# A gated decoder layer on one core: T2 in own tiles at the second turn, later stores of forced jobs, spread loads, the last multiply of the recurrence on VectorE

## The chip, the core and the metric

The kernel runs on one core of a Trainium2 chip. The metric is the device time of one execution in microseconds (us), the median of the runs. The engines of the core work through queues of their own, each in program order: TensorE (PE in the profile, with its weight loads PEld), VectorE (DVE), ScalarE (ACT), GpSimd (POOL) and SyncE (SP), which issues all of this kernel's DMAs. A wait of an instruction holds up everything behind it on its engine.

## What is computed

One layer over 2112 tokens (2048 of a prompt and 8 x 8 of running sequences) with 1024 features. The reference, cut to what matters:

```python
xn = rms_norm(x, norm_pre)
z = jnp.einsum('btd,de->bte', xn, w_in)          # 1024 -> 4096: v_pool, g_pool, u_lru, g_lru
y_pool, new_pool = pool_mixer(v_pool, ...)       # window means 2/4/8/16, minus token, 256x256 map
xs, new_conv = causal_conv(u_lru, ...)           # depthwise, width 4
y_lru, new_h = rg_lru(xs, ...)                   # gates: sigmoid of two block-diagonal maps
#   a = exp(-8 r softplus(-lam)); u = xs * gi * sqrt(1 - a*a); h = a*h + u along the tokens
mixed = jnp.concatenate([y_pool * jax.nn.silu(g_pool), y_lru * jax.nn.silu(g_lru)], axis=-1)
out = jnp.einsum('bte,ed->btd', mixed, w_out)
x + rms_norm(out, norm_post)
```

All of it is in float32. Each large product is split: an operand a is held as a high part (rounded to a format that TensorE takes in one pass) and a low part a - high, and three matmuls (high*high, high*low, low*high) make one product.

## The kernel before

**Input stage.** The tokens are taken in three macro steps m of 704 columns, each in two halves of 352. The 4096 outputs of w_in are taken in pairs of 128-blocks, called quads: (m, p, kind) with p = 0..3 and the kinds V (pool input), G (pool gate), U (recurrence input) and L (recurrence gate). For m = 0 a quad is eight plain products. For m = 1 and 2 it is seven products by a Strassen-like scheme (pid 1 to 7), each of 12 matmuls of 352 columns, whose left factors are sums of weight blocks and whose right factors are sums of the quarters of x: X11, X22, X21, T1, T2, T3, T4 (dictionary XOF: pid 6 uses T2, pid 5 T1, pid 4 T4). The order in a quad is 1, 5, (pid 4 of the quad before), 6, 3, 2, 7. In the trace the outputs are called a, e, d with the step and kind: a1V, e2L; the weights w1V, w2L. pid 1, 6, 7 and 4 write the same bank of PSUM (a) one after the other.

**Weights.** For m = 0 the four raw blocks of a quad are loaded (w_raw: wr0V...), split by ScalarE (CAST, line 833) and VectorE (line 314), used, and stored as they are in DRAM (wsd) for later steps (hi_lo with store: the store is issued LAG = 4 us behind the split). The early kinds V and G also get their four sums made in idle places of XN (s_early). For m = 1 the quads that are "late" load raw blocks once more and make the sums then (w_step); all others, and all of m = 2, load finished 512 KB tiles from wsd, six products ahead (AHEAD).

**Turns.** Between two macro steps the quarters of x are exchanged (transition): x_raw makes a difference, x_hi the high part on ScalarE, x_lo the low part on VectorE. T1, T2 and T4 are formed in the place of the staged X(0,0), one after the other. Ahead of a turn x_chain loads the tokens again for the norm (token loads, squares on ScalarE, a row of factors by a small product r<-dg,ones), loads xt and scales it.

**Order.** No engine's order is written out by hand in this stage. Chains of work are Python generators (jobs) that yield requests ("V", "A", "G" with an assumed duration, "t" for a pause, "D" for a DMA, "P" for a small product, "?" for a condition). one_slot records one product of TensorE and then grants requests that fit into the product's assumed time (SLOT) on assumed clocks; run_jobs picks the one that can start first, with TABLE_COST against a change of ScalarE's function table and OVER for what may hang over. force finishes a job at once where a product needs its result, all its requests with it, stores too. Tiles are counted: sixteen tiles of the tag "t" hold u, g, xs, xh, xl, rg, ig, w and others. Where a quad finds fewer than two free, the loop first takes the outstanding product of the quad before (pid 4), out of turn, and then an empty slot.

**Recurrence.** lru_chain ends with a multiply of the silu of the gate by the state, 704 columns, line 1249 (1254 and 1255 in the last step), on the engine that SG_ON names. combos_chain (m = 2) forms four differences of w_out for the output stage: eight sets of four loads (wo), four subtractions and four stores (wtd), with a pause of 5 us between sets.

**Output stage.** mixed is read back and multiplied by w_out by the same scheme in an order of its own; it is not touched.

Of the kernel before, what the change touches and what calls it, by code (L numbers as in the profile page):

```python
# [17 lines left out]
D = 1024  # L18
# [36 lines left out]
NBLK = 16  # L55
SLOT = 1.94
HOP = 0.2
OVER = 0.7
AHEAD = 6
TABLE_COST = 1.3  # L60
LAG = 4.0
MLAG = 2.0
XL_ON = "V"
SG_ON = "G"
X_LEAD = (6, 5)
XOF = {1: "X11", 6: "T2", 5: "T1", 7: "T3", 4: "T4", 2: "X21", 3: "X22"}
SLOTS = ("A", "B", "X11", "T1", "T2", "X22", "T3", "X21", "T4")
KINDS = {"V": 0, "G": 8, "U": 16, "L": 24}
# [3 lines left out]
def hymba_kernel(  # L72
# [24 lines left out]
    def t_done(n):  # L97
        t_live[0] -= n
# [612 lines left out]
    QUADS = []  # L711
# [29 lines left out]
    def spawn(gen, ready=None, rank=2, then=()):  # L741
        job = {"gen": gen, "ready": T[0] if ready is None else ready, "rank": rank, "then": list(then)}
        jobs.append(job)
        jobs.sort(key=lambda j: j["rank"])
        advance(job)
        return job
# [52 lines left out]
                grant(best[2], best[1])  # L799
                moved = True  # L800

    def force(job):

        while job in jobs:
            e, arg = job["req"][:2]
            if e in clock:
                grant(job, max(clock[e], job["ready"], T[0]))
            else:
                assert e != "?" or arg()
                advance(job)  # L810
# [3 lines left out]
    IDLE = [XN[:, BASE[n] + 1024 * i:BASE[n] + 1024 * (i + 1)] for n in ("X11", "T2", "T1") for i in range(2)]  # L814
    S_OF = {5: "22", 6: "11", 7: "21", 3: "12"}
    n_idle = [0]

    def w_raw(q):
        _, p, kind = q
        for n in NAMES:  # L820
            blk, h = blocks(kind, p)[int(n[0]) - 1], int(n[1]) - 1
            t = (raw_tile if n[0] == "1" else tp_tile)(f"wr{q[0]}{kind}{p}_{n}")
            w_rawt[q, n] = w_load_raw(blk, h, t)
# [7 lines left out]
    def hi_lo(hi, lo, src, store=None):  # L831
        yield "A", 0.62
        AC.copy(out=hi, in_=src)  # L833
        yield "V", 0.71
        tsub(lo, src, hi.bitcast(F32))
        if store:
            yield "t", LAG
            yield "D", 0
            nc.sync.dma_start(out=w_key(*store[1:]), in_=store[0].bitcast(F32))
# [26 lines left out]

    def s_early(q):
        def made(i):
            b = IDLE[n_idle[0] % len(IDLE)]
            n_idle[0] += 1  # L870
            early.append(spawn(hi_lo(b[:, :512], b[:, 512:], w_rawt[q, S_OF[S_PID[i]]], (b, q[2], q[1], S_PID[i])),
                               clock["V"] + HOP, rank=1))
        early.append(spawn(s_sums(q, made), rank=1))

    early = []

    def w_step(q, pid):
        m, p, kind = q
        t = w_tiles[q, pid] = half_tile(f"w{m}{kind}{p}_{pid}")
        if not is_late(q) or pid in (1, 2, 4):  # L880
            nc.sync.dma_start(out=flat_of(t).bitcast(F32), in_=w_key(kind, p, pid))
            return
        n = S_PID.index(pid)
        if n == 0:
            w_jobs[q, "s"] = {"n": 0, "job": spawn(s_sums(q, lambda i: w_jobs[q, "s"].update(n=i + 1)), rank=0)}
# [382 lines left out]
    def x_chain(m):  # L1268
        first = -(-m * MW // P)
        tiles = list(range(first, min(-(-(m + 1) * MW // P), N_TT)))  # L1270
        places = [("A", 0), ("A", 1), ("B", 0), ("B", 1)]
        for i0 in range(0, len(tiles), 4):
            part = tiles[i0:i0 + 4]
            yield "D", 0
            for i, (s_, j) in zip(part, places):
                load_tok(i, s_, j)
            yield "t", 9.0
            for i in part:
                yield "A", 1.06
# [12 lines left out]
        yield "?", lambda: t_free() >= 2  # L1292
        dg, rt = roots(m)
        for c in range(2):
            yield "A", 1.5
            r_diag(2 * m + c, dg[:, c * CW:(c + 1) * CW])
        for c in range(2):
            def rows(c=c):
                R = r_rows(2 * m + c, dg[:, c * CW:(c + 1) * CW])
                return [("A", 0.45, lambda: AC.copy(out=rt[:, c * CW:(c + 1) * CW], in_=R))]  # L1300
            yield "P", rows
        yield "t", 3.0
        for k in range(KT):
# [16 lines left out]
    def transition(m):  # L1320

        X = x_quarter
        at = {0: {"X11": -99, "T1": -99, "T2": -99, "X22": 4, "T3": 5, "X21": 7, "T4": 9},
              1: {"X11": 1, "T1": 2, "T2": 4, "X22": 5, "X21": 6, "T3": 7, "T4": 10}}[m]
        src = {"X11": X(0, 0), "T1": X(0, 0), "T2": X(0, 0), "X22": X(1, 1), "T3": X(0, 1), "X21": X(1, 0),
               "T4": X(0, 0)}
        done = set()

        def put(n, eng="V"):
            yield "?", lambda: slot_of[0] >= at[n]  # L1330
            yield "A", 1.37
            x_hi(n, src[n])
            yield eng, 3.4 if eng == "G" else 1.65
            x_lo(n, src[n], {"V": V, "G": G}[eng])
            done.add(n)

        def chain():
            yield "?", lambda: "X11" in done
            yield "V", 1.75
            x_raw(src["T1"], X(0, 1), X(0, 0))  # L1340
            x_jobs["T1"] = spawn(put("T1"), clock["V"] + HOP, rank=0)
            yield "?", lambda: "T1" in done
            yield "V", 1.75
            x_raw(src["T2"], X(1, 1), src["T1"])
            x_jobs["T2"] = spawn(put("T2"), clock["V"] + HOP, rank=0)
            yield "V", 1.75
            x_raw(src["T3"], X(1, 1), X(0, 1))
            x_jobs["T3"] = spawn(put("T3"), clock["V"] + HOP, rank=0)
            yield "?", lambda: "T2" in done
            yield "V", 1.75  # L1350
            x_raw(src["T4"], X(1, 0), src["T2"])
            x_jobs["T4"] = spawn(put("T4"), clock["V"] + HOP, rank=0)
        x_macro[0] = m + 1
        x_jobs["X11"] = spawn(put("X11"), rank=0)
        for n in ("X22", "X21"):
            x_jobs[n] = spawn(put(n), rank=0)
        x_jobs["sums"] = spawn(chain(), rank=0)
# [17 lines left out]
    def combos_chain():  # L1375
        def load(k):
            r = {}
            for i, j in ((0, 0), (1, 1), (0, 1), (1, 0)):
                r[i, j] = (raw_tile if i else tp_tile)(f"wo{k}_{i}{j}")
                nc.sync.dma_start(  # L1380
                    out=r[i, j], in_=w_out[(8 * i + k) * P:(8 * i + k + 1) * P, PIECE * j:PIECE * (j + 1)])
            return r
        nxt = load(0)
        yield "t", 6.0
        for k in range(KT):
            yield "D", 0
# [12 lines left out]

    def region_chain(r, j, k0, k1):  # L1400
        yield "D", 0
# [97 lines left out]
    with tc.manual_schedule():  # L1499
# [188 lines left out]
        for n, (qi, i, qp, pid) in enumerate(slots):  # L1688
            q = QUADS[qi]
            m = q[0]  # L1690
            if i == 0:
# [206 lines left out]
```

## Time and profile before

| | us |
|---|---|
| median of 3 runs | 1180.25 (1179.82 to 1180.95) |
| the profiled execution | 1178.76 |
| its span, first to last instruction | 1177.0 |
| mean granted clock of TensorE | 0.987 |
| DMA | 322.10 MB, mean 274 GB/s |
| of it in pieces under 2 KB | 86433 of 180537 packets |

One execution is taken apart. Its instructions have a start, a duration, the names of the tiles that they write and read, and, where the engine sat idle before one of them, the time and what ended it (in brackets: [2.18 <-ACT e L994] is 2.18 us, ended by ScalarE's write of e on line 994). Rows with an x count are several of a kind in a row. SPq rows are the issue of DMAs on SyncE, waits on the queue included. A table of windows cuts the span into stretches and gives the busy time in each. PEclk is the clock that TensorE was granted.

### The profile page before, as it was taken

How to read it: one execution, taken by the hardware profiler on the slowest of the kernel's cores; microseconds unless marked ns; L12 is line 12 of the kernel's file. 1: busy time of each engine (PE TensorE's matmuls, PEld its weight loads, DVE VectorE, ACT ScalarE, POOL GpSimd, SP SyncE). 2: the span in 40 equal slices, each digit the busy share in tenths (PEclk: the TensorE clock that was granted, in tenths of full speed). 3: DMA queues.
4: the chain of work that ended last, by engine and by line, in shares of the span. 5: the costliest groups of instructions: out<-in, count | busy, mean ns of one | idle time of the engine just before them, and what ended most of it. 6: DMA issues, size and time to landing. Idle time of an engine off the chain costs nothing. (4 is left out here: it accounts for less than half of the span.)

```text
span 1177.0 us, 17796 instructions
## 1 busy us (share of the span) xinstructions
PE 1127.4 (96%) x6274; PEld 1053.1 (89%) x6274; DVE 897.8 (76%) x1380; ACT 659.7 (56%) x1108; POOL 187.7 (16%) x248
## 2 busy tenths in 40 slices
PE   7989999999999999989799999999999999999996
PEld 6989999999999999989799988999878888888875
DVE  6768894999868777588779877657587578778777
ACT  5448759758765668647486936356664242335222
POOL 4200200100012010010211130202020003221332
PEclk9999999999999999999999989999999999999998
DMA  9367788975889999989599999988779677766563
GB/s 336 121 233 257 280 329 299 354 278 221 285 292 336 311 327 343 389 302 314 180 353 386 368 335 377 352 311 272 219 202 288 185 206 217 203 214 201 162 183 126
DMA packets 180537, 322.10 MB, mean 274 GB/s; under 512 B 24737, under 2 KB 86433, under 8 KB 180449
## 3 DMA queue, kind: packets, MB, share of 16 engines
q1 hardware_dynamic: 180448, 320.97, 79.6%
q8 instruction: 49, 0.80, 0.3%
q14 instruction: 40, 0.32, 0.1%
HBM read 218.51 MB, written 102.15 MB: 272 GB/s over the span
## 5 line engine op out<-in xcount | busy, mean ns | idle before, releaser
L451 PE MATMUL p<-XN,s 128*128 128x512 f32 (+1 forms) x224 | 86.9, 388 | 1.9 <-DVE s L139 1.9
L449 PE MATMUL p<-XN,s 128*128 128x512 f32 (+1 forms) x224 | 86.8, 388 | 1.2 <-ACT s L136 1.2
L450 PE MATMUL p<-XN,s 128*128 128x512 f32 (+1 forms) x224 | 86.8, 387 | 0.0
L442 POOL TENSOR_TENSOR xr<-ac,xr 128x512 f32<-128x512 f32 x27 | 50.9, 1904 | 211.6 <-DVE ac L582 107.1
L1172 DVE SCALAR_TENSOR_TENSOR xs<-u,parT,xs 128x704 f32<-128x704 f32 (+1 forms) x72 | 72.0, 1010 | 2.9 <-ACT xs L1161 2.7
L562 ACT ACTIVATE p<-ac 128x512 f32<-128x512 f32 (+1 forms) x32 | 18.8, 587 | 80.1 <-DVE ac L442 80.1
L245 PE MATMUL zL<-XN,wL 128*128 128x352 f32 x384 | 62.6, 322 | 0.0
L245 PEld LDWEIGHTS zL<-XN,wL 128*128 128x128 f32 x384 | 61.6, 188 | 0.0
L1135 DVE SCALAR_TENSOR_TENSOR g<-y,parT,g 128x352 f32<-128x352 f32 x48 | 27.9, 581 | 41.3 <-PE y L245 41.1
L136 ACT CAST s<-a 128x512 fp32r<-128x512 f32 x48 | 28.6, 616 | 53.3 <-DVE a L442 41.5
L442 DVE TENSOR_TENSOR a<-a,a 128x512 f32<-128x512 f32 x48 | 34.1, 716 | 30.2 <-DMA a<-mixed 27.4
L450 PE MATMUL p<-XN,a 128*128 128x512 f32 x137 | 54.2, 396 | 0.0
L449 PE MATMUL p<-XN,a 128*128 128x512 f32 x137 | 54.2, 395 | 0.0
L451 PE MATMUL p<-XN,a 128*128 128x512 f32 x137 | 54.2, 395 | 0.0
L245 PE MATMUL y<-dh,pw 128*128 128x352 f32 x192 | 54.1, 323 | 0.0
L245 PE MATMUL zV<-XN,wV 128*128 128x352 f32 x288 | 50.2, 329 | 4.0 <-ACT wV L833 3.7
L451 PEld LDWEIGHTS p<-XN,s 128*128 128x128 f32 x224 | 42.1, 188 | 12.0 <-DVE s L139 2.7
L449 PEld LDWEIGHTS p<-XN,s 128*128 128x128 f32 x224 | 42.1, 188 | 11.0 <-ACT s L136 1.7
L245 PEld LDWEIGHTS zV<-XN,wV 128*128 128x128 f32 x288 | 47.6, 193 | 4.6 <-ACT wV L833 3.9
L450 PEld LDWEIGHTS p<-XN,s 128*128 128x128 f32 x224 | 42.2, 188 | 9.5
L245 PE MATMUL zU<-XN,wU 128*128 128x352 f32 x288 | 47.7, 322 | 0.0
L245 PE MATMUL zG<-XN,wG 128*128 128x352 f32 x288 | 47.2, 323 | 0.0
(342 smaller groups left out, 3235.7 us busy)
## 6 DMA issues: line engine op xcount, KB each, us to landing
a<-mixed SPq DMA_DIRECT2D x112, 256.0 KB, 4.0
mixed<-g SPq DMA_DIRECT2D x48, 352.0 KB, 5.7
w2V<-wsd SPq DMA_DIRECT2D x28, 512.0 KB, 7.2
w2G<-wsd SPq DMA_DIRECT2D x28, 512.0 KB, 5.8
w2U<-wsd SPq DMA_DIRECT2D x28, 512.0 KB, 7.3
w2L<-wsd SPq DMA_DIRECT2D x28, 512.0 KB, 7.1
wsd<-XN SPq DMA_DIRECT2D x27, 512.0 KB, 4.8
w1V<-wsd SPq DMA_DIRECT2D x24, 512.0 KB, 5.8
```

The costliest lines, as they stand in the source:

```text
L136: hi_eng.copy(out=hi, in_=src)
L245: nc.tensor.matmul(out, lhsT=lhsT, rhs=rhs, start=start, stop=stop)
L442: (eng or nc.vector).tensor_tensor(out=out, in0=a, in1=b, op=op)
L449: nc.tensor.matmul(out, lhsT=ah, rhs=wh, start=start and k == 0, stop=False)
L450: nc.tensor.matmul(out, lhsT=ah, rhs=wl, start=False, stop=False)
L451: nc.tensor.matmul(out, lhsT=al, rhs=wh, start=False, stop=stop and k == KT - 1)
L562: nc.scalar.activation(out=junk, in_=o, func=AF.Square, accum_out=st[:, g:g + 1])
L1135: V.scalar_tensor_tensor(out=g[:, cs], in0=Y, scalar=col(C_SCALE, blk), in1=g[:, cs], op0=ALU.mult, op1=ALU.mult)
L1172: V.scalar_tensor_tensor(out=xs, in0=E[:, k:k + n], scalar=col(C_CW + 8 * k, b), in1=xs, op0=ALU.mult, op1=ALU.add)
```

## The change

- SG_ON: the last multiply of the recurrence (24 times) on VectorE.
- force takes an argument stores. Without it, it leaves a job when only a pause or a DMA is left, so that the store is issued at its own time. The stores of sums in idle places are forced where the place is used again, and at a turn.
- At the second turn T2 may be formed in two tiles of tag "t" of its own (if two are free) before T1 is split; T4 is then formed there too.
- x_chain starts one quad later at the first turn (X_LEAD), and its token loads come one by one, 3 us apart.
- Late raw loads: for m = 1, at the second product of the quad before, in place of the last product of the quad before that; their sums are planned no earlier than 5 us after the load (w_time).
- WO_PACE: 12 us between sets of w_out in place of 5.
- OVER 0.7 to 1.0 and TABLE_COST 1.3 to 1.4.

```diff
-OVER = 0.7
+OVER = 1.0
-TABLE_COST = 1.3
+TABLE_COST = 1.4
+WO_PACE = 12.0
-SG_ON = "G"
-X_LEAD = (6, 5)
+SG_ON = "V"
+X_LEAD = (5, 5)
...
-    def force(job):
+    def force(job, stores=False):
...
             e, arg = job["req"][:2]
+            if e in "tD" and not stores:
+                return
...
     def w_raw(q):
         _, p, kind = q
+        w_time[q] = T[0] + 5.0
...
     def s_early(q):
         def made(i):
-            b = IDLE[n_idle[0] % len(IDLE)]
+            n = n_idle[0] % len(IDLE)
+            b = IDLE[n]
             n_idle[0] += 1
-            early.append(spawn(hi_lo(...), clock["V"] + HOP, rank=1))
+            if n in places:
+                force(places[n], True)
+            places[n] = spawn(hi_lo(...), clock["V"] + HOP, rank=1)
+            early.append(places[n])
...
-            w_jobs[q, "s"] = {"n": 0, "job": spawn(s_sums(...), rank=0)}
+            w_jobs[q, "s"] = {"n": 0, "job": spawn(s_sums(...), max(T[0], w_time[q]), rank=0)}
...
-            yield "D", 0
             for i, (s_, j) in zip(part, places):
+                yield "D", 0
                 load_tok(i, s_, j)
-            yield "t", 9.0
+                yield "t", 3.0
+            yield "t", 5.0
...
             done.add(n)
+            if n == "T4" and t2:
+                t_done(2)
...
-            yield "?", lambda: "T1" in done
+            yield "?", lambda: "T1" in done or (m == 1 and t_free() >= 2)
+            if "T1" not in done:
+                t2.extend(t_tile(f"t2_{i}") for i in range(2))
+                src["T2"] = src["T4"] = t2
             yield "V", 1.75
             x_raw(src["T2"], X(1, 1), src["T1"])
...
         x_macro[0] = m + 1
+        for job in places.values():
+            force(job, True)
...
-            yield "t", 5.0
+            yield "t", WO_PACE
...
-            if (pid == 7 if m else i == 0) and qi + 2 < len(QUADS) and is_late(QUADS[qi + 2]):
+            if m == 0 and i == 0 and is_late(QUADS[qi + 2]):
                 w_raw(QUADS[qi + 2])
+            if m == 1 and i == 1 and is_late(QUADS[qi + 1]) and QUADS[qi + 1] not in w_time:
+                w_raw(QUADS[qi + 1])
```

How the order moves, at three places. The first is SyncE's queue at the start of the planned part: wr0L and wr0V are raw blocks of the first two quads, w_0 and w_1 the finished U blocks of the start, wL the tiles of the first L quad, lwr and pwr the maps of the recurrence and the pool. Before:

```order
L343 DMA wr0L_22_556<-in_w_in 128x512
L839 DMA wsd<-wL_11_560 128x1024
L839 DMA wsd<-wL_12_564 128x1024
L1559 DMA wsd<-w_0_472 128x1024
L1559 DMA wsd<-w_1_475 128x1024
L1559 DMA wsd<-w_1_481 128x1024
L839 DMA wsd<-wL_22_674 128x1024
L343 DMA wr0V_11_686<-in_w_in 128x512
L343 DMA wr0V_12_688<-in_w_in 128x512
L343 DMA wr0V_21_690<-in_w_in 128x512
L343 DMA wr0V_22_692<-in_w_in 128x512
L912 DMA lwr_708<-in_lru_w 128x256 x2
```

And of the change:

```order
L344 DMA wr0L_22_556<-in_w_in 128x512
L1578 DMA wsd<-w_0_472 128x1024
L1578 DMA wsd<-w_1_475 128x1024
L1578 DMA wsd<-w_1_481 128x1024
L344 DMA wr0V_11_683<-in_w_in 128x512
L344 DMA wr0V_12_685<-in_w_in 128x512
L344 DMA wr0V_21_687<-in_w_in 128x512
L344 DMA wr0V_22_689<-in_w_in 128x512
L922 DMA lwr_705<-in_lru_w 128x256 x2
L844 DMA wsd<-wL_11_560 128x1024
L844 DMA wsd<-wL_12_563 128x1024
```

The stores of the wL tiles have moved from ahead of the raw loads and lwr to behind them.

The second place is VectorE's queue at the second turn: XN are the parts of x (a row of 128x1408 is a low part of a whole quarter), XA the staged x, t_0 and t_1 the new tiles, e_2 the outputs of the first V quad of m = 2. Before, from the low part of T3 to that of T4:

```order
L314 TENSOR_TENSOR XN<-XA,XN 128x1408
L990 TENSOR_TENSOR e_2_5712<-d2V_5812,e_2_5712 128x352
L1228 SCALAR_TENSOR_TENSOR rg_4_5355<-rg_4_5355,w_4_5761 128x704
L990 TENSOR_TENSOR e_2_5715<-a2V_5718,e_2_5715 128x288
L990 TENSOR_TENSOR e_2_5715<-a2V_5718,e_2_5715 128x8x8
L1135 SCALAR_TENSOR_TENSOR g_1_5078<-y_5845,parT,g_1_5078 128x352
L314 TENSOR_TENSOR XA<-XA 128x2x352 x2
L314 TENSOR_TENSOR XN<-XA,XN 128x1408
```

Of the change, from the difference T3 to the add of the last product:

```order
L315 TENSOR_TENSOR XA<-XA 128x2x352 x2
L315 TENSOR_TENSOR XN<-t_0_5710,XN 128x704
L315 TENSOR_TENSOR XN<-t_1_5711,XN 128x704
L315 TENSOR_TENSOR t_0_5710<-XA,t_0_5710 128x704
L315 TENSOR_TENSOR t_1_5711<-XA,t_1_5711 128x704
L1000 TENSOR_TENSOR e_2_5771<-e2V_5796,e_2_5771 128x288
L1000 TENSOR_TENSOR e_2_5771<-e2V_5796,e_2_5771 128x8x8
L315 TENSOR_TENSOR XN<-XA,XN 128x1408
L1000 TENSOR_TENSOR e_2_5771<-d2V_5868,e_2_5771 128x352
L315 TENSOR_TENSOR XN<-t_0_5710,XN 128x704
L315 TENSOR_TENSOR XN<-t_1_5711,XN 128x704
L1000 TENSOR_TENSOR e_2_5774<-a2V_5777,e_2_5774 128x288
```

T4's difference has moved from behind the adds of the products a2V to ahead of the first add, and its low part from behind those adds to between them.

The third place is SyncE's queue in the last G quad of m = 1, where x of the next step is loaded (XA from in_xt) beside weights and the raw blocks of an L quad. Before, where two more loads of xt stand directly ahead of these rows:

```order
L1144 DMA mixed<-g_1_4423 128x704
L343 DMA wr1L_11_5053<-in_w_in 128x512
L343 DMA wr1L_12_5055<-in_w_in 128x512
L343 DMA wr1L_21_5057<-in_w_in 128x512
L343 DMA wr1L_22_5059<-in_w_in 128x512
L881 DMA w1G_2_5075<-wsd 128x1024
L881 DMA w1G_7_5094<-wsd 128x1024
L1284 DMA XA<-in_xt 128x2x704
L1144 DMA mixed<-g_1_4424 128x704
L881 DMA w1L_1_5114<-wsd 128x1024
L1284 DMA XA<-in_xt 128x2x704
L881 DMA w1G_4_5152<-wsd 128x1024
```

Of the change:

```order
L890 DMA w1G_2_5068<-wsd 128x1024
L1154 DMA mixed<-g_1_4413 128x704
L890 DMA w1G_7_5090<-wsd 128x1024
L344 DMA wr1L_11_5096<-in_w_in 128x512
L344 DMA wr1L_12_5098<-in_w_in 128x512
L344 DMA wr1L_21_5100<-in_w_in 128x512
L344 DMA wr1L_22_5102<-in_w_in 128x512
L890 DMA w1L_1_5118<-wsd 128x1024
L1295 DMA XA<-in_xt 128x2x704
L1270 DMA mixed<-g_1_4582 128x704
L890 DMA w1G_4_5167<-wsd 128x1024
L1295 DMA XA<-in_xt 128x2x704 x3
```

w1G_2 and w1G_7 have moved ahead of the raw loads; before, all four loads of xt stand ahead of w1G_4, now one, and three behind it.

More of the change, by code (lines that the diff above doesn't have):

```diff
@@ L816, in hymba_kernel @@
     n_idle = [0]
+    w_time = {}
     def w_raw(q):
         _, p, kind = q
+        w_time[q] = T[0] + 5.0
         for n in NAMES:
@@ L868, in made @@
         def made(i):
-            b = IDLE[n_idle[0] % len(IDLE)]
+            n = n_idle[0] % len(IDLE)
+            b = IDLE[n]
             n_idle[0] += 1
-            early.append(spawn(hi_lo(b[:, :512], b[:, 512:], w_rawt[q, S_OF[S_PID[i]]], (b, q[2], q[1], S_PID[i])),
-                               clock["V"] + HOP, rank=1))
+            if n in places:
+                force(places[n], True)
+            places[n] = spawn(hi_lo(b[:, :512], b[:, 512:], w_rawt[q, S_OF[S_PID[i]]], (b, q[2], q[1], S_PID[i])),
+                              clock["V"] + HOP, rank=1)
+            early.append(places[n])
         early.append(spawn(s_sums(q, made), rank=1))
-    early = []
+    early, places = [], {}
     def w_step(q, pid):
@@ L884, in w_step @@
         if n == 0:
-            w_jobs[q, "s"] = {"n": 0, "job": spawn(s_sums(q, lambda i: w_jobs[q, "s"].update(n=i + 1)), rank=0)}
+            w_jobs[q, "s"] = {"n": 0, "job": spawn(s_sums(q, lambda i: w_jobs[q, "s"].update(n=i + 1)),
+                                                        max(T[0], w_time[q]), rank=0)}
         box = w_jobs[q, "s"]
@@ L1327, in transition @@
         done = set()
+        t2 = []
         def put(n, eng="V"):
```

## The prediction

> **What bounds the kernel now.** Three lines of the page come first: the row of TensorE among the engines, and in the 40 slices the granted clock and the DMA share.
>
> ```profile
> PE 1127.4 (96%) x6274; PEld 1053.1 (89%) x6274; DVE 897.8 (76%) x1380; ACT 659.7 (56%) x1108; POOL 187.7 (16%) x248
> PEclk9999999999999999999999989999999999999998
> DMA  9367788975889999989599999988779677766563
> ```
>
> TensorE is busy 96% of a span of 1177.0 us and the change leaves its products as they are. So a gain can only come out of its idle time, and out of the stretches after an idle in which it runs at half clock. The table of windows (20 us each: width, busy time of PE, PEld, DVE, ACT, POOL, clock, DMA share, GB/s) says where these are:
>
> ```profile
> 80.00:100.00 20.00, 16.45 (x92) 16.16 (x93) 18.69 (x29) 14.76 (x28) 0.22 (x2) 0.91 0.75 276
> 300.00:320.00 20.00, 17.82 (x102) 17.53 (x101) 16.63 (x24) 13.37 (x21) 0.52 (x1) 0.91 0.82 264
> 480.00:500.00 20.00, 18.93 (x117) 18.30 (x115) 12.39 (x22) 10.84 (x22) 0.88 (x1) 1.00 1.03 407
> 500.00:520.00 20.00, 16.26 (x95) 15.85 (x94) 17.42 (x23) 8.78 (x17) 3.48 (x5) 0.91 0.93 341
> 540.00:560.00 20.00, 17.30 (x106) 16.47 (x104) 17.10 (x19) 16.43 (x22) 2.25 (x2) 1.00 0.96 347
> 560.00:580.00 20.00, 14.96 (x79) 14.15 (x80) 12.81 (x18) 6.26 (x8) 2.44 (x5) 0.91 0.54 170
> 680.00:700.00 20.00, 17.33 (x88) 16.33 (x87) 13.76 (x21) 5.55 (x11) 7.90 (x12) 0.83 0.97 336
> 760.00:780.00 20.00, 17.35 (x98) 17.06 (x98) 10.54 (x16) 6.47 (x12) 1.66 (x6) 0.91 0.98 373
> ```
>
> I count a window's loss as 20 minus PE's busy time, plus 20 times the clock that is missing: 5.35 at 80 (3.55 + 1.8), 3.98 at 300, 6.6 at 480 to 520, 9.5 at 540 to 580, 6.1 at 680, 4.45 at 760; together 36 us. The waits of TensorE name what ends them (total, times, longest):
>
> ```profile
> PE zV L245 <- ACT wV L833: 3.7, 1, 3.7
> PE a1V L243 <- ACT e L994: 2.2, 1, 2.2
> PE a1G L243 <- DMA w1G<-wsd: 3.7, 1, 3.7
> PE a2V L243 <- ACT XN L329: 4.5, 2, 3.7
> PE a2V L243 <- DVE XN L314: 2.5, 2, 1.2
> PE a2V L243 <- DMA w2V<-wsd: 2.1, 2, 1.9
> PE e2L L243 <- DMA w2L<-wsd: 2.6, 1, 2.6
> ```
>
> They are five places with five causes; each is taken on its own.
>
> **Place 1, 80 us: a store that holds up loads.** The rows: SyncE's longest wait, GpSimd's splits of the U weights, the issue of the lwr loads, ScalarE's wait for them, and the time from issue to landing of such a load.
>
> ```profile
> SPq L839 <- DVE wL L314: 28.3, 2, 28.1
> 42.12 6.37 POOL L314 TENSOR_TENSOR w<-wr,w 128x512 fp32r<-128x512 f32 x4 [19.23 <-ACT w L1459]
> 70.62 1.91 SPq L912 DMA_DIRECT2D lwr<-in_lru_w x2
> 76.48 0.62 ACT L928 CAST lw<-lwr 128x512 fp32r<-128x512 f32 x1 [12.23 <-DMA lwr<-in_lru_w]
> DMA to landing us min/median/max: 3.4/5.1/5.4
> ```
>
> SyncE stands 28 us at the store of wL, whose split DVE makes late; behind it wait wr0V and lwr, and for lwr ScalarE, with the cast of wV behind it. With forced jobs storing later, the order shows wsd<-w, wr0V and lwr ahead of that store. The w stores need GpSimd's splits, done at 48.5; three stores, four loads and two halves of lwr at about 0.95 us of issue each bring lwr out near 57 and in near 62, before ScalarE's idle begins at 64.25. TensorE was held for 3.65, so lwr may land as late as 72. The wait goes: **-5.35** (0 if something else holds SyncE there).
>
> **Place 2, 300 us: the first turn.** Products follow each other every 1.92 us (starts of the first two rows); the third had to wait for ScalarE's copy of the first one's bank.
>
> ```profile
> 298.37 2.08 PE L243 MATMUL a1V<-XN,w1V 128*128 128x352 f32 x12
> 300.29 2.08 PE L243 MATMUL e1V<-XN,w1V 128*128 128x352 f32 x12
> 304.06 0.43 ACT L994 COPY e<-a1V 128x352 f32<-128x352 f32 x1
> 304.55 3.00 PE L243 MATMUL a1V<-XN,w1V 128*128 128x352 f32 x12 [2.18 <-ACT e L994]
> ```
>
> The copy stands behind casts that wait for DVE. The change moves the x chain one quad later and the final multiply of the recurrence from GpSimd to DVE. Its price and its relief:
>
> ```profile
> L1249 POOL TENSOR_TENSOR g<-g,rg x16: 1692/1714/2379, 121.8 to 653.5; 128x704 f32<-128x704 f32 x16
> 292.52 0.88 DVE L1221 SCALAR_TENSOR_TENSOR w<-rg,xs 128x704 f32<-128x704 f32 x1
> 292.60 2.38 POOL L1249 TENSOR_TENSOR g<-g,rg 128x704 f32<-128x704 f32 x1
> 293.32 2.94 DVE L314 TENSOR_TENSOR wr1V<-wr1V,wr1V 128x512 f32<-128x512 f32 x2
> 296.18 0.68 DVE L314 TENSOR_TENSOR w1V<-wr1V,w1V 128x512 fp32r<-128x512 f32 x1
> ```
>
> On DVE a multiply of 704 columns costs 0.88, 24 of them 21 us. While GpSimd multiplies, two sums that take 2 x 0.68 took 2.94: DVE is held up for 1.6. The 24 hold it up for 0 to 38 us; I take about 20, since DVE is busy 76% of the time and not always with two tensors. So DVE's load stays as it is (bounds: 21 more to 17 less).
>
> Then I count DVE's rows in the changed order, from the last pool evacuation before the L quad, which is done 6.8 us before that quad begins (four products of U lie between), to the low half of w1V_7: 12 of 0.68, 6 of 0.88, 4 of 1.62 (1408 columns) and 3 differences of 1.68, 25 us, so DVE is there 18.2 us into the quad. The third product of the turn needs the copy at 19.2 (ten products). It is in time by 1 us. But w1V_4 now follows w1V_7 directly on the same bank. The trace has such a pair and DVE's add that empties the bank:
>
> ```profile
> 549.91 0.52 DVE L990 TENSOR_TENSOR g<-a1L,g 128x352 f32<-128x352 f32 x1
> 550.49 2.18 PE L243 MATMUL a1L<-XN,w1L 128*128 128x352 f32 x12 [0.66 <-DVE g L990]
> ```
>
> With DVE's queue I price it 1.1: **-2.9** (bounds: +1, the old wait with the pair, to -4).
>
> **A rule on the clock.** After waits of 2.18 and 1.9 us the trace shows clocks of 0.91 and 0.83, the first product taking 3.00 instead of 2.08. The Trainium skill ("TensorE: Matmul & The Clock Gate", Part 1) has the clock halved after an idle window of about 3.4 us; by it those two waits, and that of 2.6, would cost themselves alone, the losses 7 us less, the gain 4.7 less, and the time 1161. The trace differs, and I go by the trace.
>
> **Place 3, 500 us: DMA.** The window at 480 moves 407 GB/s at a share of 1.03. w1G_4 is waited for 3.7 us. Before, it stood behind all four loads of xt (721 KB each) and was used directly after w1G_7; now three of them are behind it (5.3 us at that rate) and two products stand in between (3.8 us); w1G_2 stands ahead of four raw loads. That is 9 us of slack for waits of 3.7 and 0.8, and the token loads are 3 us apart. I leave 0.8: **-5.8** (bounds 0 to -6.6).
>
> **Place 4, 560 us: the second turn.** T4 was made last:
>
> ```profile
> 570.61 1.68 DVE L314 TENSOR_TENSOR XA<-XA 128x704 f32<-128x704 f32 x2
> 573.72 1.62 DVE L314 TENSOR_TENSOR XN<-XA,XN 128x1408 fp32r<-128x1408 f32 x1 [1.43 <-ACT XN L329]
> ```
>
> Now T2 is formed in its own tiles before T1 is split. From the start of w1L_7, DVE's rows are: its evacuation (at 2.2, 0.5), two low parts (3.2), T3 (1.7), T2's low part (1.7): done at 9.3, its first half at 8.5. TensorE reaches w2V_6 at 7.7 and waits 0.8. T4's difference ends at 11. Behind it come the evacuation after w2V_3, T3's low part (14.9; needed at 14.4) and T4's low part at 17.1; w2V_4 is due at 16.8 but follows w2V_7 directly, whose evacuation stands behind T4's part: 1.0. Left are 2.3 of 9.5: **-7.2** (bounds -3 to -9).
>
> **Place 5, 680 and 760 us: DMA again.** One row on what comes with a V quad, two loads of st_pool in pieces of 15 numbers, and the window without w_out loads:
>
> ```profile
> 746.32 3.55 SPq L957 DMA_DIRECT2D e<-in_st_pool x2
> 780.00:800.00 20.00, 20.00 (x127) 20.00 (x126) 13.68 (x20) 16.65 (x23) 1.09 (x2) 1.00 0.83 270
> ```
>
> WO_PACE moves the eight sets of w_out (2.1 MB each with the stores) from behind 30, 32, 40, 47, 51, 60, 65, 73 of the 112 w2 loads to behind 27, 29, 36, 48, 54, 65, 74, 81. From the third set on that is 0.32 and then 0.23 MB per 0.52 MB weight load; at 2.2 us each, 380 and then 340 GB/s, where full windows move 373 to 407. But up to the V quad at 680 as many sets are loaded as before, with one directly ahead of st_pool. I leave 4 there and 1 at 760: **-5.5** (bounds +3 to -10.5).
>
> **What comes in.** The order takes w1V_4 out of turn in the second V quad too: T tiles are short there, and the next G quad's copy on ScalarE must wait for the recurrence to free one. Behind it in ScalarE's queue are casts and copies of other banks; TensorE waits for that bank two products later, 3.8 us that hide most of it: **+1** (0 to 5). For queues that I could not follow: **+2** (0 to 8). The raw loads of late quads come two products later, w_time 5 us behind them, OVER and TABLE_COST only reorder; nothing, since their splits are issued six products ahead of use (AHEAD); without that cover they are part of the 8.
>
> **The sum.** -5.35 - 2.9 - 5.8 - 7.2 - 5.5 + 1 + 2 = -23.75. The profiled execution took 1178.76, which gives 1155.0; the median of the runs is 1.5 above it: **1156.5 us**.
>
> **Rivals.** (a) The DMA engines are the bound from 480 to 780 whatever the spread: the bytes stay. For it: shares of 0.93 to 1.03 in those windows. Places 3 and 5 stay, and the sum is 11.3 less: 1168. (b) Everything named goes and nothing comes: 36 us, 1144. (c) DVE becomes what TensorE waits for: if GpSimd's multiplies were no hindrance, DVE has 21 us more, its evacuations queue in order, and each late one costs 0.88 and up to 1.8 of half clock, 2.7. For it: 18.69 of 20 busy at 80. From ten such places on, 27 us, the gain is gone: 1156.5 + 27, about 1183. Against it: the 2.94 row. (d) The order does not deliver: T2's tiles are taken only with two T tiles free. The order shows t_0 and t_1 written, so what is left of this is that each wait only moves elsewhere: near 1179.
>
> **Chances.** Forecast 0.62 (1148 to 1164); (a) 0.17; (b) 0.11; (c) 0.06; (d) 0.04. A measurement tells 0.2% from no change, 2.4 us. Faster 0.9, same 0.04, slower 0.06. The range holds the forecast, (a) to its end and the near part of (b): 1145 to 1171.
>
> **What would show it.** Right: no ACT wait for lwr and full PE to 100 us; no copy wait at 300 and a short one at w1V_4; no w1G wait; the T4 wait down to 1 us; POOL's L1249 rows gone and DVE's busy time within 10 us of 897.8. Wrong: PE waits on DVE in new places, w2 loads waited for as long as now, or a wait of some 4 us in the second G quad.

## The result and the profile after

The changed kernel takes 1161.82 us (median of four runs, 1158.19 to 1163.41) against 1180.6 for the kernel before; the ratio is 0.9833, interval 0.9805 to 0.9861. It is faster by 1.7%. The profiled execution took 1163.41 us (span 1161.7), 15.35 less than the profiled one of before. The forecast was 1156.5.

From the page after, TensorE's row, its clock and the DMA share:

```profile
PE 1118.8 (96%) x6274; PEld 1046.0 (90%) x6274; DVE 894.7 (77%) x1414; ACT 661.3 (57%) x1110; POOL 160.7 (14%) x216
PEclk9999999999999999999899999999999999999998
DMA  9565987976998979996899999997789567766553
```

TensorE does the same 6274 matmuls. To see where the 15 us came from, one set of windows over both kernels. The columns are those of the windows in the prediction, and the number to look at is the count of TensorE's matmuls (the first x). Before:

```profile
70.00:100.00 30.00, 26.00 (x152) 25.42 (x151) 21.45 (x34) 18.25 (x32) 0.22 (x2) 0.94 0.72 259
340.00:380.00 40.00, 40.00 (x251) 40.00 (x251) 28.73 (x41) 25.78 (x38) 4.11 (x6) 1.00 0.91 322
420.00:460.00 40.00, 40.00 (x252) 40.00 (x251) 36.61 (x51) 24.48 (x39) 4.68 (x7) 1.00 0.95 341
480.00:520.00 40.00, 35.19 (x210) 34.15 (x209) 29.82 (x44) 19.63 (x38) 4.36 (x6) 0.96 0.98 374
540.00:600.00 60.00, 52.26 (x309) 50.62 (x308) 47.20 (x58) 35.12 (x50) 10.46 (x14) 0.97 0.77 272
680.00:780.00 100.00, 92.98 (x536) 89.75 (x535) 66.16 (x99) 44.26 (x73) 19.75 (x40) 0.95 0.99 362
```

And after:

```profile
70.00:100.00 30.00, 30.00 (x189) 30.00 (x188) 21.88 (x33) 21.25 (x36) 0.42 (x3) 1.00 0.63 232
300.00:320.00 20.00, 18.92 (x119) 18.63 (x118) 16.71 (x25) 9.20 (x15) 3.24 (x7) 1.00 0.88 322
340.00:380.00 40.00, 38.67 (x240) 38.14 (x239) 31.27 (x45) 29.65 (x43) 6.20 (x7) 1.00 0.85 287
420.00:460.00 40.00, 37.75 (x235) 37.17 (x234) 31.95 (x45) 27.25 (x44) 3.59 (x6) 1.00 0.86 310
480.00:520.00 40.00, 37.70 (x228) 37.21 (x227) 31.70 (x49) 26.49 (x49) 3.41 (x5) 0.96 1.01 386
540.00:600.00 60.00, 50.39 (x293) 49.26 (x292) 43.13 (x58) 30.83 (x48) 6.49 (x15) 0.91 0.86 290
680.00:780.00 100.00, 97.69 (x607) 96.98 (x606) 80.73 (x124) 60.30 (x93) 13.76 (x29) 1.00 1.01 383
```

A 40 us window in which TensorE never waits holds 251 matmuls (340 to 380 before), 0.1594 us each. A window's loss is its width less 0.1594 for each matmul in it (300 to 320 before, shown above, had 102). Differences are taken before rounding. This counts a wait and the half clock behind it once each. The prediction's count, idle plus missing clock, counts a long wait twice when the clock is already halved within it; at 540 after it would give 15.0 in place of 13.3. Losses in us, and the prediction's terms:

| Window | Before | After | Change | Forecast |
|---|---|---|---|---|
| 70 to 100 (place 1) | 5.8 | 0 | -5.8 | -5.35 |
| 300 to 320 (place 2) | 3.7 | 1.0 | -2.7 | -2.9 |
| 480 to 520 (place 3) | 6.5 | 3.7 | -2.9 | -5.8 |
| 540 to 600 (place 4) | 10.7 | 13.3 | +2.6 | -7.2 |
| 680 to 780 (place 5) | 14.6 | 3.2 | -11.3 | -5.5 |
| 340 to 380 (T shortage) | 0 | 1.7 | +1.7 | +1 |
| 420 to 460 (unplaced) | 0 | 2.5 | +2.5 | +2 |

The changes add up to -15.9; the profiled executions differ by 15.35. So the table holds nearly all of it. Places 1 and 2 came as forecast, place 4 got worse, and place 5 gave twice what was forecast. Its window is wider than the two of 20 us that the prediction counted: between them, from 700 to 760, the kernel before lost some 3.5 us that the prediction hadn't counted. What TensorE waits for now (total, times, longest; rows of the start and of the output stage are left out):

```profile
PE e2V L244 <- DVE XN L315: 7.3, 1, 7.3
...
PE a1G L244 <- DVE g L1000: 4.5, 2, 2.3
...
PE e2G L244 <- ACT g L1004: 1.4, 1, 1.4
PE a1G L244 <- ACT g L1004: 1.3, 1, 1.3
PE a2L L244 <- ACT rg L1212: 1.3, 1, 1.3
PE a1V L244 <- DVE e L1000: 1.1, 1, 1.1
```

Of the waits of before for w1G, w2V, w2L, wV and the copy of e none is left. New are waits for VectorE: 7.3 us for e2V at the second turn, and 4.5 in two pieces for a1G at 436 and 502. The order in time around the first of them, VectorE (two parts of its timeline), TensorE, and SyncE's issue:

```profile
543.38 1.69 DVE L315 TENSOR_TENSOR t<-XA 128x704 f32<-128x704 f32 x2
544.99 0.52 DVE L1000 TENSOR_TENSOR g<-e1L,g 128x352 f32<-128x352 f32 x1
551.53 0.89 DVE L1231 SCALAR_TENSOR_TENSOR w<-rg,xs 128x704 f32<-128x704 f32 x1 [6.02 <-DMA mixed<-g]
...
557.94 3.60 PE L244 MATMUL e2V<-XN,w2V 128*128 128x352 f32 x11 [7.26 <-DVE XN L315]
...
543.88 0.44 SPq L1154 DMA_DIRECT2D mixed<-g  x1
```

VectorE stands for 6.02 us at the first write of w, a step of the recurrence that nobody waits for. That write needs a T tile. T2 has just taken the last two long-free ones (the two rows of t), so w gets the tile of g whose store was issued at 543.88. The store lands at 551.5, some 7.6 us later. Behind w, in order, stand the low parts that e2V needs.

### The profile page after: what moved, and what is told of

Its sections match the earlier page's. It is cut to its first block, busy times and chain, and to the rows that moved or that the text cites. A ratio compares the mean times of both kernels' runs of the same rounds, so it can differ in the third digit from the quotient of the medians.

```text
span 1161.7 us, 17810 instructions
## 1 busy us (share of the span) xinstructions
PE 1118.8 (96%) x6274; PEld 1046.0 (90%) x6274; DVE 894.7 (77%) x1414; ACT 661.3 (57%) x1110; POOL 160.7 (14%) x216
## 5 line engine op out<-in xcount | busy, mean ns | idle before, releaser
L1182 DVE SCALAR_TENSOR_TENSOR xs<-u,parT,xs 128x704 f32<-128x704 f32 (+1 forms) x72 | 67.9, 955 | 3.1 <-ACT xs L1171 2.8
```

The lines of the kernel that those rows point to most:

```text
L1182: V.scalar_tensor_tensor(out=xs, in0=E[:, k:k + n], scalar=col(C_CW + 8 * k, b), in1=xs, op0=ALU.mult, op1=ALU.add)
```

## The experiments

All ratios are to the kernel before, run beside each experiment on the same chip: its medians were 1177.7 us for experiments 1 to 4, 1179.05 for 5 to 8, and 1177.56 for 9 to 11 and the repetition of 2. The expectations name such a group a "call".

**1. w later in VectorE's queue.** The tile stays, only the place of the row moves:

```diff
+        if (m, b) == (1, 5):
+            yield "t", 8.0
         yield "V", 0.92
         u = t_chain(f"w{m}_{b}")[:, :n]
```

> The changed kernel with the first write of w for block 5 of m = 1 planned 8 us later; its tile is still the one whose store is under way, so only its place in VectorE's queue moves, behind T2's low parts. Theory (VectorE stands 6.0 us at that write for the store, with the low parts of T2 behind it): the 7.3 us wait of e2V goes to 1 or less, the loss of the turn (550 to 574 us) from 11.7 to 4 or less, the time from 1161.8 to 1153 to 1156. Rival (the turn is bound by the DMA engines or by the order of the casts, the place of w does not matter): TensorE waits the same 7 us somewhere in the turn, the time stays at 1160 to 1163.

Measured: 1169.58 us, ratio 0.9935 (0.9909 to 0.9962), so slower than the changed kernel. The turn itself did what the theory says. e2V waits 1.7 in place of 7.3. The windows from 540 to 572 and from there to 600:

```profile
540.00:572.00 32.00, 29.41 (x181) 28.57 (x180) 26.72 (x34) 21.17 (x29) 2.43 (x5) 1.00 0.87 305
572.00:600.00 28.00, 21.23 (x118) 20.64 (x117) 20.65 (x28) 13.88 (x25) 9.54 (x8) 0.88 0.86 288
```

And the timeline at 580, on ScalarE and TensorE:

```profile
580.29 0.62 ACT L1429 CAST XA<-wb 128x512 fp32r<-128x512 f32 x1 [6.33 <-DMA wb<-in_w_out]
581.32 3.89 PE L244 MATMUL e2G<-XN,w2G 128*128 128x352 f32 x12 [5.80 <-ACT g L1004]
```

Loss to 572: 3.1, against 10.5 in the changed kernel (135 matmuls). But the planner filled the room otherwise: ScalarE now stands 6.33 us at a cast for a late load of w_out, the copy of g is behind it, and 572 to 600 loses 9.2. From 540 to 600 that is 12.3, little less than the 13.3 of the changed kernel; what makes this run slower than that kernel lies elsewhere (2.5 us more from 680 to 780, and waits in the output stage). Half of the theory (the stall at w makes the wait of e2V) is shown; its price for the whole is not, since the new order carries a wait of the same kind elsewhere.

**2. T2 in place again.**

```diff
-            yield "?", lambda: "T1" in done or (m == 1 and t_free() >= 2)
+            yield "?", lambda: "T1" in done or (m == 1 and t_free() >= 99)
```

> The changed kernel with T2 formed in place again, as before. Theory (T2's tiles take the last two free T tiles, and w gets one whose store is under way): VectorE's 6.0 us wait for mixed<-g is gone, but T4 comes last again with its wait of about 3.7 us and those of 1 to 1.5 for T2; the loss of the turn is 9 to 12 us as in both kernels, the time 1160 to 1164. Rival (the tiles of T2 gain what was forecast, 7.2 us, and the 6 us stall comes from elsewhere and stays): 1167 to 1170.

Measured: 1152.14 us, ratio 0.9789 (0.9756 to 0.9821), repeated beside experiments 9 to 11:

> The run without T2's tiles once more, as the base of the three others of this call. Its ratio to before was 0.9789 and that of the changed kernel 0.983 twice. If T2's own tiles cost time here, the ratio is 0.976 to 0.981 again; if the first measurement was luck, 0.982 to 0.985.

1153.40 us, 0.9787 (0.9772 to 0.9802). The changed kernel has 0.9833 and 0.983 (below), so without T2's tiles it is about 5 us faster. On the time both the theory (no change) and the rival (7 us slower) missed. From the repeated run, the window of the turn:

```profile
540.00:600.00 60.00, 57.10 (x352) 56.06 (x351) 48.21 (x63) 33.69 (x50) 7.96 (x15) 1.00 0.94 335
```

And the two rows of VectorE's timeline that answer to those above:

```profile
544.90 0.88 DVE L1231 SCALAR_TENSOR_TENSOR w<-rg,xs 128x704 f32<-128x704 f32 x1
546.38 0.53 DVE L1000 TENSOR_TENSOR g<-e1L,g 128x352 f32<-128x352 f32 x1 [0.60 <-PE e1L L244]
```

w is written without a wait, and the loss of the turn is 3.9, not 9 to 12. So the turn of the changed kernel no longer needed T2's tiles. Why shows in TensorE's rows. Before, the product that uses T4 (pid 4) came out of turn, directly behind pid 7 (566.61):

```profile
573.75 0.43 PE L243 MATMUL a2V<-XN,w2V 128*128 128x352 f32 x1 [3.67 <-ACT XN L329]
```

In the repeated run it comes in turn, behind two products of the next quad, and doesn't wait:

```profile
569.28 2.08 PE L244 MATMUL e2G<-XN,w2G 128*128 128x352 f32 x12
571.20 2.08 PE L244 MATMUL a2V<-XN,w2V 128*128 128x352 f32 x12
```

What is left of the turn's waits is 1.6 us for the low part of T3 and 1.2 for that of T2. In the changed kernel pid 4 comes directly behind pid 7 again (573.50). The loop takes it out of turn where T tiles are short, and two of them hold T2 there; that this is the reason was not tested by itself. A second difference is that in the kernel before the evacuations of three pool maps (559.80, 564.89 and 570.11) stood in VectorE's queue between the parts of T, and here none does.

**3. Raw loads as early as before.**

```diff
-            if m == 0 and i == 0 and is_late(QUADS[qi + 2]):
+            if (pid == 7 if m else i == 0) and qi + 2 < len(QUADS) and is_late(QUADS[qi + 2]):
                 w_raw(QUADS[qi + 2])
-            if m == 1 and i == 1 and is_late(QUADS[qi + 1]) and QUADS[qi + 1] not in w_time:
-                w_raw(QUADS[qi + 1])
```

> The changed kernel with the raw blocks of the late quads of m = 1 loaded at the time of before, a product of the last quad but one. T2's tiles are then not free, so T2 is formed in place as in the run without its tiles; that run is the one to compare with. Theory (raw blocks come late, VectorE waits 5.0 and 4.3 us for them, does the sums in one crowd, and its adds of a1G come 2.2 and 2.3 us late at 436 and 502): these two waits go, the time is 5 to 7 us below that of the run without T2's tiles. Rival (the crowd is the recurrence with its multiplies on VectorE): the two waits stay, the time is within 2 us of that run.

Measured: 1163.01 us, 0.9895 (0.9844 to 0.9946), 11 us above the run that it was to be 5 to 7 below. Of the two waits for a1G none is left, as the theory has it, but others come. From 480 to 520 the loss is still 3.5 (229 matmuls), where TensorE now waits 2.2 us for VectorE's xl. Most of the 11 us lies later: 320 matmuls from 540 to 600 against 353 in run 2, and 583 from 680 to 780 against 625, with a wait of 2.4 for w2U. The theory holds for the two waits and fails for the sum.

**4. The multiplies on GpSimd, replanned.**

```diff
-SG_ON = "V"
+SG_ON = "G"
```

> The changed kernel with the 24 final multiplies of the recurrence on GpSimd again. Theory (what they cost on VectorE they cost there as hold-up): VectorE's busy time stays within 6 us of 894.7, the time within 3 us of 1161.8. Rival 1 (the multiplies make VectorE late for a1G): the waits at 436 and 502 go, 1155 to 1158. Rival 2 (GpSimd's hold-up is what held the first turn): a wait of 2 us for the copy near 300 is back, 1165 or more.

Measured: 1171.68 us, 0.995 (0.9932 to 0.9969). VectorE's busy time is 892.5, within 6 of 894.7, as the theory has it. The time is 10 us up, and some 14 by the ratios (0.995 against 0.9833, each with its own runs of the kernel before), as rival 2 would have it, but not by its mechanism: no wait for the copy near 300 is back. The planner sees a longer multiply and makes another order, with a 5.4 us wait for a1G near 500; the window from 480 to 520 has 153 matmuls, a loss of 15.6. Hence experiment 10, which moves nothing else.

**5. The changed kernel once more.**

> The changed kernel itself, to have it on the same chip and beside the same runs of the kernel before as the three others of this call. Its ratio to before was 0.9833; 0.981 to 0.986 is expected, and its 7 us wait of e2V with VectorE's 6 us wait for the store of mixed is there again, if that wait belongs to the order; by the rival, that it was an accident of the DMA engines in one execution, it is gone or below 3 us.

Measured: 1158.58 us, 0.983 (0.9802 to 0.9859). e2V waits 8.9 us and VectorE 7.7 for the store: the wait belongs to the order. The store lands 9.3 us after its issue here, in place of 7.6, and the wait is longer by as much.

**6. Forced jobs store at once.**

```diff
-    def force(job, stores=False):
+    def force(job, stores=True):
```

> The changed kernel with forced jobs storing at once, as before. VectorE's order is that of the changed kernel row for row; on SyncE the stores of wL stand ahead of wr0V and lwr again. Theory (that store holds lwr, ScalarE and with it TensorE): SyncE waits some 28 us at the store of wL, TensorE 3 to 4 us for zV near 80, loss there 5 to 6; the time is 4 to 7 us above that of the changed kernel in this call. Rival (lwr is held by something else of the start, and the place of the stores is of no matter): no wait near 80, within 2 us.

Measured: 1164.06 us, 0.987 (0.9843 to 0.9896), 5.5 us above run 5. From the waits, SyncE's at the store of wL and TensorE's for wV:

```profile
SPq L844 <- DVE wL L315: 34.5, 6, 27.8
...
PE zV L246 <- ACT wV L838: 3.8, 1, 3.8
```

And the window:

```profile
70.00:100.00 30.00, 25.84 (x152) 25.25 (x151) 21.49 (x34) 18.28 (x32) 0.22 (x2) 0.94 0.71 258
```

152 matmuls, as before the change: the loss of 5.8 is back, and with it the wait at the store of wL. The edit moves all forced stores; the two rows name this one. The intervals of the two times overlap, so it is the window and the rows that show place 1, not the time.

**7. The old pace of w_out.**

```diff
-WO_PACE = 12.0
+WO_PACE = 5.0
```

> The changed kernel with 5 us between the sets of w_out, as before. Theory (the pace took the weight waits away): waits for w2 loads come back between 680 and 780, loss there 6 to 13 us in place of 2.9, the time 4 to 10 us above that of the changed kernel in this call. Rival (they went because the other edits moved the V quad and its st_pool loads, not through the pace): losses there up to 4, the time within 2 us.

Measured: 1172.51 us, 0.995 (0.9922 to 0.9977), 13.9 above run 5 and more than the theory's 10. The window has 528 matmuls, a loss of 15.8:

```profile
680.00:780.00 100.00, 88.93 (x528) 87.27 (x527) 65.66 (x101) 45.78 (x73) 15.88 (x26) 0.97 0.96 340
```

The row that moves with it is one of SyncE's waits: the loads of a set of w_out wait for the stores of an earlier one, whose tiles they take. With 5 us (SyncE's row, and TensorE's longest wait for a weight):

```profile
SPq L1399 <- DMA wtd<-wo: 24.4, 16, 3.7
PE a2V L244 <- DMA w2V<-wsd: 4.4, 1, 4.4
```

In the kernel before:

```profile
SPq L1380 <- DMA wtd<-wo: 20.9, 12, 2.7
```

And in the changed kernel:

```profile
SPq L1399 <- DMA wtd<-wo: 1.3, 4, 0.3
```

The spread of the bytes hardly differs: the loads of the eight sets are issued from 615.9 to 732.0 us before, from 607.2 to 731.5 in the changed kernel and from 610.7 to 719.7 here. Full DMA engines alone don't explain the waits either: at a share of 1.04, run 7 loses 6.8 us from 720 to 740 (411 GB/s), and the changed kernel nothing from 700 to 720 (407 GB/s). So the pace is shown as the cause; that it works through SyncE's waits rests on these rows, since no run moves those waits alone.

**8. More time ahead of the first difference of w_out.** In run 2 VectorE waits 4.3 us for such a load at 608.

```diff
+            yield "?", lambda: "T1" in done or (m == 1 and t_free() >= 99)
...
         nxt = load(0)
-        yield "t", 6.0
+        yield "t", 12.0
```

> The run without T2's tiles (1152.1, ratio 0.9789), with 12 us in place of 6 between the first loads of w_out and their first difference. There VectorE waited 4.3 us for such a load at 608, and TensorE 3.8 for VectorE's add at 617, loss 5.6. Theory (the wait in order on VectorE makes that loss): both are gone, the ratio is 0.974 to 0.976. Rival (VectorE's queue is full there anyway, the add comes late without the load): a wait of 2 us or more near 615 stays, 0.978 to 0.980.

Measured: 1159.26 us, 0.9837 (0.9811 to 0.9862). The loss from 600 to 640 falls from 5.6 to 0.8 (216 and 246 matmuls), as the theory says, but all sets of w_out now come later, and waits for w2U, pw and w2L between 705 and 754 take it back: 580 matmuls from 680 to 780, a loss of 7.5 where run 2 has 0.4. By the ratios the run is some 6 us slower than run 2.

**9. The reciprocal root split.** In the changed kernel VectorE's rows ahead of the late add of a1G are these:

```profile
501.28 0.19 DVE L290 RECIPROCAL tok<-tok 128x6 f32<-128x6 f32 x1 [1.61 <-ACT tok L289]
...
501.99 0.52 DVE L1000 TENSOR_TENSOR g<-a1G,g 128x352 f32<-128x352 f32 x1
```

The edit, beside T2 in place:

```diff
         yield "V", 0.2
-        yield "A", 0.3, "sqrt"
-        tok_rsqrt(tiles[0], tiles[-1] + 1)
-        clock["V"] = max(clock["V"], clock["A"]) + 0.5
-        yield "t", 0.8
+        V.tensor_scalar(out=ms, in0=ms, scalar1=1.0 / D, scalar2=EPS, op0=ALU.mult, op1=ALU.add)
+        yield "A", 0.3, "sqrt"
+        AC.activation(out=r, in_=ms, func=AF.Sqrt)
+        yield "V", 0.8
+        V.reciprocal(out=r, in_=r)
...
```

> The run without T2's tiles, with the reciprocal root of the tokens in three planned steps in place of one. On VectorE four short rows (the reciprocal and what follows it) move behind the add of a1G near 500; TensorE's and ScalarE's orders stay. Theory (VectorE stands 1.6 us at the reciprocal for ScalarE's root, directly ahead of that add): TensorE's wait for a1G near 500 falls from 2.3 to 3.7 us to 1.3 or less, the loss there from 4 to 5 us to 2 or less, the time 2 to 4 us below the base of this call. Rival (the add is late because the sums of the raw blocks that came late crowd VectorE): the wait stays above 2, the time within 1.5 us of the base.

Measured: 1153.42 us, 0.98 (0.9784 to 0.9817), the same as the base. The wait for a1G near 500 is gone altogether, and TensorE, earlier by that much, stands further on for ScalarE's copy behind a late raw load:

```profile
509.53 0.69 DVE L318 TENSOR_TENSOR wr1U<-wr1U,wr1U 128x512 f32<-128x512 f32 x1 [2.47 <-DMA wr1U<-in_w_in]
510.30 0.62 ACT L838 CAST w1U<-wr1U 128x512 fp32r<-128x512 f32 x1 [5.20 <-DVE wr1U L318]
514.61 1.71 PE L244 MATMUL a1L<-XN,w1L 128*128 128x352 f32 x9 [2.10 <-ACT g L1004]
```

The theory is right on the wait and wrong on the time.

**10. The multiplies executed on GpSimd in an unchanged order** (T2 in place):

```diff
-        SGE = {"V": V, "G": G}[SG_ON]
+        SGE = G
```

> The run without T2's tiles, planned with the 24 multiplies on VectorE, but executed on GpSimd: nothing else moves on any engine. Theory (a multiply holds VectorE up on GpSimd for about as long as it takes on VectorE): VectorE's busy time stays within 6 us of the base, though 21 us of multiplies are gone from it, and the time within 2 us. Rival 1 (the hold-up is smaller, VectorE gains room): busy time 10 or more below, time 2 to 5 us below the base. Rival 2 (the hold-up hits rows that TensorE waits for): time 3 or more above.

Measured: 1155.96 us, 0.9822 (0.9786 to 0.9857), with a spread from 1149.82 to 1166.5; not told apart from the base. VectorE's busy time, here and in the base:

```profile
PE 1119.8 (97%) x6274; PEld 1048.2 (91%) x6274; DVE 898.5 (78%) x1380; ACT 660.2 (57%) x1107; POOL 203.7 (18%) x248
```

```profile
PE 1118.5 (97%) x6274; PEld 1047.5 (91%) x6274; DVE 896.0 (78%) x1412; ACT 661.0 (57%) x1107; POOL 156.4 (14%) x216
```

24 multiplies (32 rows, the last 8 in two parts) are gone from VectorE, and it is 2.5 us busier. In the base they take 16 of 0.886 and 8 of 0.818 and 0.22, 22.5 us, so from GpSimd they hold VectorE up by some 25 (two executions of one kernel differ by 0.5 to 2.7 us in VectorE's busy time). The Trainium skill ("GPSIMD Engine Reference", 1. Specifications) has GpSimd's SBUF interfaces shared with VectorE, with contention where a VectorE instruction has two SBUF inputs; this pair of runs agrees and gives it a size, about 1 us for each multiply.

**11. Token loads in one piece, the x chain a quad earlier** (T2 in place):

```diff
-X_LEAD = (5, 5)
+X_LEAD = (6, 5)
...
+            yield "D", 0
             for i, (s_, j) in zip(part, places):
-                yield "D", 0
                 load_tok(i, s_, j)
-                yield "t", 3.0
-            yield "t", 5.0
+            yield "t", 9.0
```

> The run without T2's tiles, with the four token loads of a group in one piece and the x chain of m = 1 one quad earlier, as before. Theory (the spread and the place of these loads freed the weights of the last G quad, and the later chain freed the first turn): a wait for DMA w1G near 500 of 2 us or more, or one for the copy of e near 300 of 1.5 or more, is back; the time is 3 to 9 us above the base of this call. Rival (other edits did that: the raw loads that come later, or the multiplies off GpSimd): neither wait is back, the time within 2 us.

Measured: 1159.39 us, 0.9839 (0.9826 to 0.9853), 6 us above the base, as much as the theory said but not as it said. No wait for w1G is back, and the copy near 300 is waited for 0.5 at most, as the rival has it; its time is not the rival's. In their place a raw load lands late, and VectorE with ScalarE behind it holds a1G:

```profile
494.00 0.69 DVE L318 TENSOR_TENSOR wr1L<-wr1L,wr1L 128x512 f32<-128x512 f32 x1 [10.01 <-DMA wr1L<-in_w_in]
498.73 3.89 PE L244 MATMUL a1G<-XN,w1G 128*128 128x352 f32 x12 [4.53 <-ACT g L1004]
```

## Why the prediction held, and where it did not

The time lies in the range, 5.3 us above the forecast, and in the direction forecast. But two terms were off by more than that whole error, and partly cancelled, so that the sum came so near is partly luck. It is luck too that the time lies next to the 1161 of the paragraph on the clock: by the table the difference lies in places 4 and 5, not in the half clock.

- **Place 1, right.** -5.35 forecast, -5.8 found, and run 6 brings it back by undoing that one part.
- **The multiplies, right.** Forecast as neutral (21 us for about 20 of hold-up), found 22.5 for 25, VectorE's busy time 894.7 after 897.8.
- **Place 2, right in size** (-2.9, found -2.7), with the wait at w1V_4 of 1.1 that was priced. The cause is left open. The prediction named the later chain and the multiplies off GpSimd. Run 4 puts the multiplies back on GpSimd and run 11 the chain back to its old place, and in neither is the old wait back; run 11 lost 1.4 us more there.
- **Place 3, the waits gone as forecast, the term mis-sized.** The waits for w1G went, but by which edit is not shown: with the raw loads early again (run 3) and with the token loads in one piece and the chain earlier (run 11) they are not back either. The step left out what would be late next: the sums of raw blocks, moved behind late loads, and the root of the tokens stand ahead of the add of a1G. 2.9 in place of 5.8. The prediction put the later raw loads at nothing "since their splits are issued six products ahead of use"; that holds for the splits and not for VectorE's other rows behind them. Runs 3 and 9 each take the wait away, so both parts share in it.
- **Place 4, the step that failed.** "Now T2 is formed in its own tiles before T1 is split" counted VectorE's rows of x and the evacuations, each with its operands ready. It did not ask where the two tiles come from, and who gets the next one. The next is w, and it waits for a store. -7.2 became +2.6. The mechanism forecast does exist: T4 is waited for no longer (the product at 573.50 comes 0.7 us late, behind no engine that the profile names), and with the stall out of the way in run 1 the loss to 572 is 3.1. But run 2 shows that the rest of the change brings the turn to 3.9 by itself.
- **Place 5, right in direction, mis-sized by half.** It was priced by bandwidth (340 GB/s in place of 380). The windows of the changed kernel move more, 383 GB/s at a share of 1.01, with TensorE hardly waiting. What held the weights was, as far as the rows show, SyncE: 20.9 us at loads of w_out for the stores ahead of them. That row is in the waits of the kernel before, and the prediction did not use it.
- **What comes in:** 340 to 380 lost 1.7 where 1 was priced, for ScalarE's copy of a1G as said. It stands behind activations in a full queue; that the T tile is its root was not tested. The 2.5 at 420 is of the size of the 2 unplaced.
- **Rivals.** (a), DMA as the bound whatever the spread, falls with run 7: the same bytes at another pace cost 13.9 us more. (b), 36 us and nothing new, falls with place 4. (c), VectorE burdened by the multiplies, falls with run 10. (d), each wait only moving elsewhere, is refuted for the whole by the gain of 1.7%, though runs 1, 3, 8 and 9 do much of that. That waits appear on VectorE in new places was named as a sign of error, and it came, but from a tile's store and from late loads, not from load on the engine.

The fastest version among the runs is the changed kernel with T2 in place: 0.9789 and 0.9787 against 0.9833 and 0.983. The lower bound of the changed kernel's interval in run 5 and the upper one of the repeated run meet at 0.9802, so some 5 us is the best estimate and not a sharp one.

## What to carry to other kernels

When an edit takes a buffer early, ask which instruction gets the next buffer, what is still using it (a store that was only issued counts as using), and what stands behind that instruction on its engine; a wait that nobody needs can hold everything behind it. For a queue that issues both loads and stores, read its own waits before pricing a stretch by bandwidth. And the time is no test of a mechanism where a planner sets the order: three edits here (runs 1, 8 and 9) removed or cut the wait that they were made for and gave the gain back to others, so look at the row itself, and test with an edit that moves nothing else.

## What was not expected of the hardware

The clock's answer to a wait of 2.2 to 2.5 us is not the same from run to run. The same row in the changed kernel, and in the run without T2's tiles, whose VectorE rows up to there are the same:

```profile
438.40 2.19 PE L244 MATMUL a1G<-XN,w1G 128*128 128x352 f32 x12 [2.19 <-DVE g L1000]
```

```profile
438.20 3.16 PE L244 MATMUL a1G<-XN,w1G 128*128 128x352 f32 x12 [2.19 <-DVE g L1000]
```

After 2.19 us of waiting the product took 2.19 us, near full speed, in the one and 3.16 in the other; from 420 to 460 the clock was 1.00 against 0.96, and 235 matmuls against 226, 1.4 us. In run 10 the product after a wait of 2.51 took 2.18, and that after 2.20 took 3.70. So the length of such a wait alone does not decide, and a window that differs by 1.5 us between two kernels need not mean anything. The Trainium skill ("TensorE: Matmul & The Clock Gate", Part 1) has the clock halved after an idle window of about 3.4 us, and calls the window free-running. A phase that differs from run to run would fit these rows; that waits of only 2.2 us are enough does not fit the idle window that it states.

One store of 352 KB landed 7.6 and 9.3 us after its issue in two executions of the changed kernel, and VectorE's wait for it was 6.0 and 7.7, with the same order on VectorE each time. In run 6 the store took 7.4, but VectorE came to the row 3.9 us after the issue in place of 1.6, and waited 3.5.
